# A two-layer hybrid attention network: squares and weight halves on VectorE, products of zeros ahead of the data, gates summed in four products

## The chip, the cores and the metric

The kernel runs on one core of a Trainium2 chip. TensorE (PE in the profile) multiplies matrices into PSUM, VectorE (DVE), ScalarE (ACT) and GpSimd (POOL) work on tiles, and SyncE (SP) and ACT issue the DMAs that bring data from HBM into SBUF. Each engine takes its own instructions in order and waits on semaphores of the others. The metric is the device time of one execution in microseconds (us); lower is better.

## The reference

A sequence of 512 tokens with 1024 features passes two layers, all in float32. Each layer is an attention with three groups of heads and then a convolutional feed-forward net:

```python
def rmsnorm(x, g):
    return x * rsqrt(mean(x * x, axis=-1) + EPS) * g

for i in range(2):
    h = rmsnorm(x, ln1_g[i]) @ w_in[i]            # 1024 -> 2724 columns
    fq, fk, fv, ff, dq, dk, dv, c_q, c_kv, k_r = split(h)
    # fox: 4 heads of 64, causal; bias cum[q] - cum[k],
    #      cum = cumsum over tokens of log_sigmoid(ff + f_bias): the forget gates
    # diff: 4 heads, softmax(q1 k1) v - lam * softmax(q2 k2) v, then a norm
    # mla: 4 heads, queries and keys from two low-rank latents, rotary part
    x = x + concat(o_fox, o_diff, o_mla) @ w_o[i]
    up = causal_dwconv(rmsnorm(x, ln2_g[i]) @ w_up[i])   # 1024 -> 2 x 2816, width 3
    x = x + (silu(up[:, :2816]) * up[:, 2816:]) @ w_down[i]
return rmsnorm(x, final_g)
```

## The kernel before

The activations lie transposed in eight tiles x0 to x7, 128 features by 512 tokens each. To keep float32 accuracy on fast products, every operand is split into a high half (`hi`, a copy on ACT in the reduced format) and a low half (`lo`, the rest, subtracted on DVE or POOL); `mm3` then makes three products: hi by hi, hi by lo, lo by hi. Weights come from HBM as float32 chunks (`raw`, three buffers) and are cut into pieces whose halves are called `whi` and `wlo`. `weights()` hands out the next piece and keeps the cutting two pieces ahead (`CUT_AHEAD`); four buffers each of `whi` and `wlo` turn. The second half of each `w_fm` chunk has its `wlo` made by POOL, every other `wlo` is DVE's (line 298).

A norm is not applied ahead of the product. `Norm.halves` splits x times its column factors; the factor of each token (one over the root of the mean square) is multiplied in afterwards. For it, ACT squares each x tile (`sq`), POOL adds the eight squares (`square`), TensorE sums over partitions with a column of ones (`inv_rms`, tile `at<-ones,r`), DVE and POOL take the root (`vn`, `rsn`), TensorE spreads the factors over partitions with transposes (`spread`) and ACT copies them (tile `r`, `rb`).

The program of a layer: `tm(w_fx)` computes the fox values, the gates and the rotary keys, token by token, 292 columns wide: eight slices k of x, each with four token tiles and three products, 96 in all. At the start of layer 0 each slice waits for its DMA, its halves and its weights. Then come two projections of 24 products 512 wide (`stacked_queries`, `stacked_keys`), `tm(w_dv)` with 96 such products, in which `cumulate` puts the gates' sums, and the remaining projections, woven between the steps of the heads. The weaving follows a planner (`Plan`) that holds a cost for each operation and takes up the step whose inputs it believes ready; its costs differ for DVE and POOL, so moving an operation also changes the order in which the heads' steps stand. After the heads, the last two products per output tile are added to x (`x<-mm,x`), each followed by `halves` and `square` for the next norm. The feed-forward part starts with two tiles (`raw`, each 24 products) before the norm's factors must be there.

PSUM has eight banks: three `mm`, two `sc`, two `at`, one `o`. In the profile nearly all instructions carry line L133, the planner's helper (L135 in the changed kernel); they are told apart by their tiles.

## Time and profile before

| | us |
|---|---|
| median of 3 runs (1241.84 to 1244.34) | 1241.91 |
| the profiled execution | 1244.5 |
| its span, first to last instruction | 1242.7 |
| PE busy | 1210.6 |
| DVE busy | 815.0 |
| ACT busy | 665.0 |
| POOL busy | 288.4 |

The rows below come from that one execution. The span is 1.8 us shorter than the execution's time. A row names the engine, the line, the operation and the tiles (written<-read); "x24" counts instructions. PEld is TensorE's loading of weights, which runs beside PE. A wait is put down to the engine that released it last.

### The profile page before, as it was taken

To read this page: it belongs to the slowest core of one execution; us is meant where nothing else is said; L and a number is where in the kernel's file an instruction comes from. 1 tells how busy PE (TensorE), PEld (TensorE's weight loads), DVE (VectorE), ACT (ScalarE), POOL (GpSimd) and SP (SyncE) were. 2 spreads that over 40 slices of the span, in tenths; PEclk is the share of its full clock that TensorE was granted. 3 is DMA by queue.
4 is the path that set the end of the run, shared out by engine and by line. 5 is a ranking of instruction groups with operands and counts; after the bars stand their busy time and mean duration, and the time that the engine had idled before them with its cause. 6 is when DMAs were issued, how large, how long until landed. Compare 5 with 4: busy or idle time off the path is not lost.

```text
span 1242.7 us, 16525 instructions
## 1 busy us (share of the span) xinstructions
PE 1210.6 (97%) x5792; PEld 1010.2 (81%) x5792; DVE 815.0 (66%) x1632; ACT 665.0 (54%) x1323; POOL 288.4 (23%) x378
## 2 busy tenths in 40 slices
PE   6999999999999999999999999999999999999997
PEld 6878877878888888888898788788788888888886
DVE  5578778687665357665554887887767643666743
ACT  5477777565543245444454776875545422454524
POOL 4165353141110001111123636322211100011102
PEclk8999999999999999999999999999999999999999
DMA  5211110222222332223232111113222233222231
GB/s 208 94 68 69 56 51 26 95 78 95 99 92 83 98 119 102 86 86 94 86 115 82 69 65 44 48 38 102 86 102 98 68 101 124 87 100 102 86 118 68
DMA packets 34356, 108.33 MB, mean 87 GB/s; under 512 B 3808, under 2 KB 3936, under 8 KB 34272
## 3 DMA queue, kind: packets, MB, share of 16 engines
q1 hardware_dynamic: 33984, 106.81, 25.8%
q8 instruction: 45, 0.74, 0.2%
q10 hardware_dynamic: 288, 0.47, 0.1%
q14 instruction: 39, 0.32, 0.1%
HBM read 105.16 MB, written 2.10 MB: 86 GB/s over the span
## 4 chain that ended last, share of the span: by engine, by line
PE 86%; DVE 6%; POOL 3%; ACT 2%; issue 2%; DMA 0%; POOLq 0%; DVEq 0%; ACTq 0%
PE mm L133 75%; PE sc L133 5%; PE at L133 4%; DVE a L133 2%; PE o L133 2%; POOL rq L133 1%; POOL wlo L133 1%; DVE row L133 1%; DVE wlo L133 1%; DVE w L133 1%; ACT a L133 1%; DVE x L133 1%; POOL row L133 1%; ACT row L133 0%; ACT u L133 0%
## 5 line engine op out<-in xcount | busy, mean ns | idle before, releaser
L133 PE MATMUL mm<-a,whi 128*128 128x512 f32 x2800 | 872.5, 392 | 4.4 <-DVE a L133 4.4
L133 PEld LDWEIGHTS mm<-a,whi 128*128 128x128 f32 x2800 | 520.7, 188 | 108.7 <-DVE a L133 5.8
L133 PE MATMUL mm<-a,wlo 128*128 128x512 f32 x1400 | 546.1, 390 | 0.0
L133 ACT ACTIVATE whi<-raw 128x512 fp32r<-128x512 f32 (+3 forms) x426 | 248.9, 585 | 373.2 <-PE mm L133 323.9
L133 DVE TENSOR_TENSOR wlo<-raw,whi 128x512 fp32r<-128x512 f32 (+3 forms) x396 | 260.6, 660 | 132.2 <-ACT whi L133 127.2
L133 PEld LDWEIGHTS mm<-a,wlo 128*128 128x128 f32 x1400 | 262.9, 188 | 54.4
L133 POOL TENSOR_TENSOR a<-w,a 128x512 fp32r<-128x512 f32 x44 | 57.2, 1300 | 540.6 <-ACT a L133 521.4
L133 DVE SCALAR_TENSOR_TENSOR w<-u,par_sb,w 128x511 f32<-128x511 f32 (+1 forms) x176 | 132.1, 750 | 32.0 <-ACT w L133 28.9
L133 DVE TENSOR_TENSOR u<-mm,r 128x512 f32<-128x512 f32 x88 | 60.9, 692 | 107.3 <-PE mm L133 107.3
L133 ACT ACTIVATE a<-w 64x512 fp32r<-64x512 f32 (+1 forms) x124 | 78.4, 632 | 43.4 <-DVE w L133 41.8
L133 ACT ACTIVATE w<-u,par_sb 128x512 f32<-128x512 f32 x88 | 71.9, 817 | 33.1 <-DVE u L133 33.1
L133 POOL TENSOR_SCALAR row<-row,rsum 128x512 f32<-128x512 f32 (+1 forms) x96 | 58.0, 607 | 134.1 <-DVE rsum L133 132.4
L133 ACT ACTIVATE row<-row,nm 128x512 f32<-128x512 f32 (+1 forms) x96 | 53.8, 561 | 24.7 <-DVE nm L133 24.6
L133 PE MATMUL sc<-a 128*128 128x512 f32 (+7 forms) x288 | 66.9, 337 | 0.0
L133 DVE TENSOR_TENSOR x<-mm,x 128x512 f32<-128x512 f32 x64 | 43.9, 688 | 32.8 <-PE mm L133 32.5
L133 PE MATMUL mm<-whi,a 128*128 128x512 f32 (+2 forms) x176 | 56.1, 367 | 8.8 <-ACT whi L133 6.5
L133 POOL TENSOR_TENSOR r<-r,w 128x512 f32<-128x512 f32 x28 | 41.7, 1489 | 93.0 <-ACT w L133 92.0
L133 POOL TENSOR_TENSOR wlo<-raw,whi 128x512 fp32r<-128x512 f32 x30 | 39.9, 1329 | 82.2 <-ACT whi L133 82.1
L133 DVE TENSOR_TENSOR pl<-at,ph 128x128 fp32r<-128x128 f32 (+1 forms) x96 | 45.7, 484 | 7.8 <-ACT ph L133 7.0
L133 PEld LDWEIGHTS sc<-a 128*128 128x128 f32 (+1 forms) x288 | 46.2, 191 | 5.5 <-DVE nm L133 0.8
L133 ACT ACTIVATE ph<-at 128x128 fp32r<-128x128 f32 (+1 forms) x96 | 40.6, 433 | 15.7 <-PE at L133 11.3
L133 PE MATMUL at<-c_sb,row 128*128 128x128 f32 x240 | 43.0, 278 | 4.5 <-POOL row L133 1.9
(139 smaller groups left out, 1075.5 us busy)
## 6 DMA issues: line engine op xcount, KB each, us to landing
raw<-in_w_up SPq DMA_DIRECT2D x88, 512.0 KB, 3.2
raw<-in_w_fm SPq DMA_DIRECT2D x30, 512.0 KB, 3.2
raw<-in_w_dn SPq DMA_DIRECT2D x24, 384.0 KB, 3.0
raw<-in_w_dn SPq DMA_DIRECT2D x24, 320.0 KB, 2.8
raw<-in_w_o SPq DMA_DIRECT2D x16, 384.0 KB, 2.9
raw<-in_w_dv SPq DMA_DIRECT2D x8, 512.0 KB, 3.2
raw<-in_w_dn SPq DMA_DIRECT2D x8, 512.0 KB, 3.5
raw<-in_w_fx SPq DMA_DIRECT2D x8, 292.0 KB, 3.7
```

The costliest lines, as they stand in the source:

```text
L133: return real(*args, **kw)
```

## The change

Seven edits:

- All `wlo` are made by DVE, and so are the sums of squares; POOL keeps neither.
- Ahead of any data DVE clears a tile `rest`, and TensorE makes eight products of zeros (512 wide) into the `o` bank.
- The first norm's column factors come by a DMA of their own (`g_sb`, 4 KB) at the place of the whole parameter block; that block (`par_sb`) and the constants (`c_sb`) are issued by SP after the `w_fx` products are recorded. x1 and the second weight chunk are issued by ACT, behind its table load and first copy.
- Squares are no longer tied to the halves. In `tm(w_fx)` they come from slice 4 on; the rest of them stand in the first projection, and the sums and the spreading come later in it than before.
- The accumulators of `tm(w_fx)` take banks sc, sc, o, mm.
- The feed-forward part makes three tiles first (two in sc, one in mm), with four squares after slice 3 of the first, four after its slice 7, the sums in slice 1 and the spreading in slice 6 of the third.
- The gates' running sums take four products per layer, 16, 12, 8 and 4 columns wide, in slice 5, at the place of ten products of 4 columns in slices 1 to 4.

```diff
--- before.py
+++ after.py
@@ -45,6 +45,8 @@
 FM_ORDER = [0, 2, 1, 3, 4, 8, 5, 9, 6, 10, 12, 13, 14, 7, 11]
 CUT_AHEAD, CUT_BUFS = 2, 4
 WIDTH, SLACK = 2, -1.5
+
+WARM = 8
 
 
 def lam_init_of(l):
@@ -229,13 +231,16 @@
 
         x = [cp.tile([P, S], F32, name=f"x{j}") for j in range(KD)]
         c_sb = cp.tile([P, NCST], F32, name="c_sb")
+        g_sb = cp.tile([P, KD], F32, name="g_sb")
         par_sb = cp.tile([P, NPAR], F32, name="par_sb")
         mhalf = cp.tile([P, NT], F32, name="mhalf")
         ones = cp.tile([P, 2], F32, name="ones")
 
+        nc.scalar.dma_start(g_sb, par[:, O_LN1:O_LN1 + KD])
+        rest = A()
+        nc.vector.memset(rest.bitcast(F32), 0.0)
         nc.gpsimd.memset(ones, 1.0)
         nc.gpsimd.memset(mhalf, -0.5)
-        nc.scalar.dma_start(par_sb, par)
         warm = small(2, "warm")
         nc.scalar.activation(warm, ones, AF.Copy)
 
@@ -269,19 +274,21 @@
         pieces = [(i, sum(ws[:b]), w) for i, (_, ws) in enumerate(chunks) for b, w in enumerate(ws)]
         state = {"load": 0, "cut": 0, "use": 0}
 
-        def load():
+        def load(queue=nc.sync):
             src, ws = chunks[state["load"]]
             raw = plan.tile("raw", 3, lp.tile([P, 1024], F32, name="raw", tag="raw"))[:, :sum(ws)]
             plan.written[raw.tensor.name] = plan.written[raw.tensor.name][0] + 3.6, "DVE"
-            nc.sync.dma_start(raw, src)
+            queue.dma_start(raw, src)
             raws[state["load"]] = raw
             state["load"] += 1
 
         for j in range(KD):
-            nc.sync.dma_start(x[j], xT[j * P:(j + 1) * P, :])
-            if j in (0, 2, 4):
-                load()
-        nc.sync.dma_start(c_sb, cst)
+            (nc.scalar if j == 1 else nc.sync).dma_start(x[j], xT[j * P:(j + 1) * P, :])
+            if j in (0, 1, 3):
+                load(nc.scalar if j == 1 else nc.sync)
+        idle = o_ps()
+        for _ in range(WARM):
+            nc.tensor.matmul(idle, lhsT=rest[:, :P], rhs=rest, start=True, stop=True)
 
         def ahead():
 
@@ -295,8 +302,7 @@
                 else:
                     hi, lo = (plan.tile(v, CUT_BUFS, lp.tile([P, S], F32R, name=v, tag=v, bufs=CUT_BUFS))[:, :w] for v in ("whi", "wlo"))
                 nc.scalar.activation(hi, src, AF.Copy)
-                eng = nc.gpsimd if off and chunks[i][0].tensor.name == w_fm.tensor.name else nc.vector
-                eng.tensor_tensor(out=lo, in0=src, in1=hi.bitcast(F32), op=ALU.subtract)
+                nc.vector.tensor_tensor(out=lo, in0=src, in1=hi.bitcast(F32), op=ALU.subtract)
                 ready.append((hi, lo))
                 state["cut"] += 1
 
@@ -360,7 +366,7 @@
             def halves(self, j):
                 self.xs.append(split(x[j], scale=self.g(j)))
 
-            def square(self, eng=None):
+            def square(self):
                 j = self.squares
                 self.squares += 1
                 sq = R() if j == 0 else W()
@@ -368,18 +374,19 @@
                 if j == 0:
                     self.acc = sq
                 else:
-                    (eng or nc.gpsimd).tensor_tensor(out=self.acc, in0=self.acc, in1=sq, op=ALU.add)
+                    nc.vector.tensor_tensor(out=self.acc, in0=self.acc, in1=sq, op=ALU.add)
 
             def ready(self, k):
 
                 while len(self.xs) <= min(k, KD - 1):
                     self.halves(len(self.xs))
-                    if len(self.xs) > 2:
-                        self.square()
+
+            def squares_to(self, n):
+                while self.squares < n:
+                    self.square()
 
             def sums(self):
-                while self.squares < KD:
-                    self.square()
+                self.squares_to(KD)
                 self.rs = inv_rms(self.acc, D, "n")
 
             def spread(self):
@@ -587,8 +594,8 @@
                     return ps
                 return f
 
-            def tm(w, width, between=lambda k: None):
-                acc = [mm_ps(), mm_ps(), sc_ps(), sc_ps()]
+            def tm(w, width, banks, between=lambda k: None):
+                acc = [bank() for bank in banks]
                 for k in range(KD):
                     norm.ready(k + 1)
                     hi, lo = weights(width, w)
@@ -607,11 +614,15 @@
 
 
             norm.ready(0)
-            acc = tm(w_fx, TMX)
+            acc = tm(w_fx, TMX, (sc_ps, sc_ps, o_ps, mm_ps), lambda k: norm.squares_to(max(0, k - 3)))
+            if l == 0:
+                nc.sync.dma_start(par_sb, par)
+                nc.sync.dma_start(c_sb, cst)
             first = stacked_queries(FM_ORDER[0])
+            next(first), norm.squares_to(KD)
+            next(first), next(first)
+            norm.sums()
             next(first)
-            norm.sums()
-            next(first), next(first)
             norm.spread()
             for _ in first:
                 pass
@@ -649,14 +660,12 @@
             cum_ps = at_ps()
 
             def cumulate(k):
-                qt = k - 1
-                if not 0 <= qt < NT:
+                if k != 5:
                     return
-                for t in range(qt + 1):
-                    c = C_TRI if t == qt else C_ONE
-                    nc.tensor.matmul(cum_ps[:, 4 * qt:4 * qt + 4], lhsT=c_sb[:, c:c + P], rhs=lf[:, 4 * t:4 * t + 4], start=t == 0, stop=t == qt)
-                if qt == NT - 1:
-                    nc.vector.tensor_copy(cum, cum_ps[:, 0:nz])
+                nc.tensor.matmul(cum_ps[:, 0:nz], lhsT=c_sb[:, C_TRI:C_TRI + P], rhs=lf, start=True, stop=False)
+                for t in range(1, NT):
+                    nc.tensor.matmul(cum_ps[:, 4 * t:nz], lhsT=c_sb[:, C_ONE:C_ONE + P], rhs=lf[:, 0:nz - 4 * t], start=False, stop=t == NT - 1)
+                nc.vector.tensor_copy(cum, cum_ps[:, 0:nz])
 
             def rotate(dst, src, cs, sn, shape, name):
 
@@ -680,7 +689,7 @@
             rotate(krr.rearrange("p (t o d) -> p t o d", t=NT, o=1), kr.rearrange("p (t o d) -> p t o d", t=NT, o=1), cs4, sn4, [P, NT, 1, hf], "ro")
 
 
-            acc = tm(w_dv, S, cumulate)
+            acc = tm(w_dv, S, (mm_ps, mm_ps, sc_ps, sc_ps), cumulate)
             dv = []
             for t in range(NT):
                 dv.append(split(acc[t], scale=rs1[:, t:t + 1]))
@@ -917,35 +926,36 @@
                     mm3(ps, (hi[:, c], lo[:, c]), oT[6 + k], k == 0, k == 1)
                 nc.vector.tensor_tensor(out=x[j], in0=ps, in1=x[j], op=ALU.add)
                 nxt.halves(j)
-                nxt.square()
             return nxt
 
         def ffn(l, norm):
             last = l == DEPTH - 1
             nxt = None if last else Norm(lambda j: col(l + 1, O_LN1, j))
+            made = {}
+
+            def raw(ft, gu, bank=mm_ps, between={}):
+
+                ps = made[ft, gu] = bank()
+                for k in range(KD):
+                    if k % 4 == 0:
+                        hi, lo = weights(S, w_up)
+                    c = slice(k % 4 * P, (k % 4 + 1) * P)
+                    mm3(ps, (hi[:, c], lo[:, c]), norm.xs[k], k == 0, k == KD - 1)
+                    if k in between:
+                        between[k]()
+
+
+            raw(0, 0, sc_ps, {3: lambda: norm.squares_to(4), 7: lambda: norm.squares_to(KD)})
+            raw(0, 1, sc_ps)
+            raw(1, 0, mm_ps, {1: norm.sums, 6: norm.spread})
             for half in range(2):
                 hT = []
                 for ft in range(half * HALF, (half + 1) * HALF):
-                    y2, tiles = [], []
-
-                    def raw(ps):
-                        for k in range(KD):
-                            if k % 4 == 0:
-                                hi, lo = weights(S, w_up)
-                            c = slice(k % 4 * P, (k % 4 + 1) * P)
-                            mm3(ps, (hi[:, c], lo[:, c]), norm.xs[k], k == 0, k == KD - 1)
-                            if ft == 0 and k == 3 and len(tiles) == 2:
-                                norm.spread()
-
+                    y2 = []
                     for gu in range(2):
-                        if len(tiles) == gu:
-                            tiles.append(mm_ps())
-                            raw(tiles[-1])
-                        if norm.rb is None:
-                            norm.sums()
-                            tiles.append(mm_ps())
-                            raw(tiles[-1])
-                        ps = tiles[gu]
+                        if (ft, gu) not in made:
+                            raw(ft, gu)
+                        ps = made[ft, gu]
                         a = U()
                         nc.vector.tensor_tensor(out=a, in0=ps, in1=norm.rb, op=ALU.mult)
                         y = W()
@@ -1009,7 +1019,7 @@
                 nc.vector.tensor_scalar(out=xt[t, 1], in0=xt[t, 1], scalar1=rs, scalar2=None, op0=ALU.mult)
                 nc.sync.dma_start(out[t * P:(t + 1) * P, S:D], xt[t, 1])
 
-        norm = Norm(lambda j: col(0, O_LN1, j))
+        norm = Norm(lambda j: g_sb[:, j:j + 1])
         for l in range(DEPTH):
             norm = attention(l, norm)
             norm = ffn(l, norm)
```

Where instructions stand before and after, by engine. First DVE in `tm(w_fx)` of layer 0, from the low half of slice 5 on (a: low halves of x; wlo: low halves of weights; vn: start of the root). Before:

```order
L133 SCALAR_TENSOR_TENSOR a_235<-x5_99,par_sb_103,a_234 128x512
L133 SCALAR_TENSOR_TENSOR a_260<-x6_100,par_sb_103,a_259 128x512
L133 SCALAR_TENSOR_TENSOR a_283<-x7_101,par_sb_103,a_282 128x512
L133 TENSOR_TENSOR wlo_244<-raw_146,whi_243 128x292
L133 TENSOR_TENSOR wlo_267<-raw_146,whi_266 128x292
L133 TENSOR_TENSOR wlo_292<-raw_193,whi_291 128x512
L133 TENSOR_TENSOR wlo_327<-raw_241,whi_326 128x512
L133 TENSOR_SCALAR vn_347<-at_342 128x4
```

and now, where r is the sum of squares and w a square:

```order
L135 SCALAR_TENSOR_TENSOR a_238<-x5_99,g_sb_103,a_237 128x512
L135 TENSOR_TENSOR r_247<-r_247,w_269 128x512
L135 TENSOR_TENSOR wlo_244<-raw_157,whi_243 128x292
L135 SCALAR_TENSOR_TENSOR a_262<-x6_100,g_sb_103,a_261 128x512
L135 TENSOR_TENSOR r_247<-r_247,w_294 128x512
L135 TENSOR_TENSOR wlo_266<-raw_157,whi_265 128x292
L135 SCALAR_TENSOR_TENSOR a_285<-x7_101,g_sb_103,a_284 128x512
L135 TENSOR_TENSOR r_247<-r_247,w_313 128x512
L135 TENSOR_TENSOR wlo_291<-raw_199,whi_290 128x512
L135 TENSOR_TENSOR r_247<-r_247,w_343 128x512
L135 TENSOR_TENSOR wlo_310<-raw_199,whi_309 128x512
```

Before, three slices' low halves stood ahead of the weights' of slices 6 and 7, and the sums were on POOL; now the weights' halves alternate with the slices, and the sums lie between them on the same engine.

Second DVE where layer 0's attention ends and its feed-forward part begins (a_3338 and a_3353, now a_3328 and a_3340, are the low halves of slices 6 and 7). Before:

```order
L133 SCALAR_TENSOR_TENSOR a_3319<-x5_99,par_sb_103,a_3318 128x512
L133 TENSOR_TENSOR x7_101<-mm_3344,x7_101 128x512
L133 SCALAR_TENSOR_TENSOR a_3338<-x6_100,par_sb_103,a_3337 128x512
L133 TENSOR_TENSOR wlo_3363<-raw_3221,whi_3362 128x512
L133 SCALAR_TENSOR_TENSOR a_3353<-x7_101,par_sb_103,a_3352 128x512
L133 TENSOR_TENSOR wlo_3379<-raw_3221,whi_3378 128x512
L133 TENSOR_TENSOR wlo_3407<-raw_3290,whi_3406 128x512
L133 TENSOR_SCALAR vn_3399<-at_3394 128x4
```

and now:

```order
L135 SCALAR_TENSOR_TENSOR a_3312<-x5_99,par_sb_104,a_3311 128x512
L135 TENSOR_TENSOR x7_101<-mm_3331,x7_101 128x512
L135 SCALAR_TENSOR_TENSOR a_3328<-x6_100,par_sb_104,a_3327 128x512
L135 TENSOR_TENSOR wlo_3347<-raw_3228,whi_3346 128x512
L135 SCALAR_TENSOR_TENSOR a_3340<-x7_101,par_sb_104,a_3339 128x512
L135 TENSOR_TENSOR r_3362<-r_3362,w_3364 128x512
L135 TENSOR_TENSOR wlo_3374<-raw_3228,whi_3373 128x512
L135 TENSOR_TENSOR r_3362<-r_3362,w_3367 128x512
L135 TENSOR_TENSOR wlo_3405<-raw_3286,whi_3404 128x512
L135 TENSOR_TENSOR r_3362<-r_3362,w_3370 128x512
L135 TENSOR_TENSOR wlo_3421<-raw_3286,whi_3420 128x512
```

The halves and x keep their order; the sums of squares (r_3362), which stood on POOL beside these, follow the last slice's half on DVE.

Third TensorE in `tm(w_dv)`, the last of the gates' sums (lf: logarithms of the gates; at: their sums). Before (groups of one, two and three stand in the three slices ahead of it):

```order
L133 MATMUL sc_489<-whi_509,a_187 128x512
L133 MATMUL sc_490<-whi_509,a_186 128x512
L133 MATMUL sc_490<-wlo_510,a_186 128x512
L133 MATMUL sc_490<-whi_509,a_187 128x512
L133 MATMUL at_475<-lf_472,c_sb_102 128x4 x4
L133 MATMUL mm_487<-whi_528,a_211 128x512
```

and now, the only group:

```order
L135 MATMUL sc_503<-whi_540,a_217 128x512
L135 MATMUL sc_503<-wlo_541,a_217 128x512
L135 MATMUL sc_503<-whi_540,a_218 128x512
L135 MATMUL at_488<-lf_485,c_sb_102 128x16
L135 MATMUL at_488<-lf_485,c_sb_102 128x12
L135 MATMUL at_488<-lf_485,c_sb_102 128x8
L135 MATMUL at_488<-lf_485,c_sb_102 128x4
L135 MATMUL mm_500<-whi_556,a_237 128x512
```

Ten products became four, one slice later. Beyond these places, the order of the heads' steps among the projections differs from the fox heads on, since the planner's view of DVE and POOL has changed.

## Rows read from the trace of the kernel before

**Rows 1.** The page, section 1: busy us (share of the span) xinstructions.

```profile
PE 1210.6 (97%) x5792; PEld 1010.2 (81%) x5792; DVE 815.0 (66%) x1632; ACT 665.0 (54%) x1323; POOL 288.4 (23%) x378
```

**Rows 2.** What TensorE waited for, whole span: us in total, times, longest us.

```profile
PE mm L133 <- DVE a L133: 4.8, 3, 2.2
PE mm L133 <- DVE wlo L133: 3.1, 1, 3.1
```

**Rows 3.** Stages of the start: us, busy (x) by engine, PEclk, DMA share, GB/s.

```profile
6.40:11.40 5.00, 4.95 (x20) 4.95 (x21) 4.47 (x7) 5.00 (x11) 2.28 (x2) 1.00 1.06 405
11.40:17.20 5.80, 5.80 (x44) 5.57 (x42) 5.80 (x5) 5.39 (x12) 5.00 (x5) 1.00 0.65 254
17.20:22.40 5.20, 1.74 (x12) 1.50 (x11) 5.20 (x5) 1.18 (x3) 4.75 (x3) 0.92 0.21 80
22.40:28.40 6.00, 5.99 (x24) 6.00 (x25) 1.62 (x3) 0.63 (x1) 0.00 (x0) 0.50 0.49 178
```

**Rows 4.** Timeline of the start: start us, us, instruction xcount [idle before <-releaser].

```profile
0.72 0.10 POOL L133 MEMSET ones<- 128x2 f32 x1 [0.29 <-POOLq L1068]
...
4.82 0.72 ACT L133 ACTIVATE a<-x,par_sb 128x512 fp32r<-128x512 f32 x1 [2.17 <-DMA par_sb<-in_par]
...
5.45 0.61 ACT L133 ACTIVATE r<-x 128x512 f32<-128x512 f32 x1
...
6.45 0.86 PE L133 MATMUL mm<-whi,a 128*128 128x292 f32 x2 [6.45 <-ACT whi L133]
...
7.38 0.75 DVE L133 SCALAR_TENSOR_TENSOR a<-x,par_sb,a 128x512 fp32r<-128x512 f32 x1
...
13.90 6.46 POOL L133 TENSOR_TENSOR r<-r,w 128x512 f32<-128x512 f32 x4 [0.47 <-ACT w L133]
...
15.76 5.15 DVE L133 SCALAR_TENSOR_TENSOR a<-x,par_sb,a 128x512 fp32r<-128x512 f32 x3
...
22.41 0.61 PE L133 MATMUL mm<-wlo,a 128*128 128x292 f32 x1 [3.07 <-DVE wlo L133]
```

**Rows 5.** The same timeline of TensorE, further on.

```profile
28.17 0.75 PE L133 MATMUL mm<-a,whi 128*128 128x512 f32 x2
```

**Rows 6.** DMA issues, first 22 us: xcount, KB each, median us to landing.

```profile
x<-in_xT SPq DMA_DIRECT2D x8, 256.0 KB, 5.3
...
c_sb<-in_cst SPq DMA_DIRECT2D x1, 832.0 KB, 7.1
par_sb<-in_par ACTq DMA_DIRECT2D x1, 200.0 KB, 4.1
```

**Rows 7.** Timeline, DVE, where layer 0's attention meets its feed-forward half.

```profile
264.32 1.78 DVE L133 TENSOR_TENSOR wlo<-raw,whi 128x512 fp32r<-128x512 f32 x1
266.02 1.74 DVE L133 SCALAR_TENSOR_TENSOR a<-x,par_sb,a 128x512 fp32r<-128x512 f32 x1
```

**Rows 8.** The same stretch, POOL.

```profile
257.14 10.08 POOL L133 TENSOR_TENSOR r<-r,w 128x512 f32<-128x512 f32 x6 [0.87 <-ACT w L133]
```

**Rows 9.** The same stretch, TensorE.

```profile
267.82 0.50 PE L133 MATMUL mm<-a,whi 128*128 128x512 f32 x1 [2.22 <-DVE a L133]
```

**Rows 10.** Chain that ended last, 40 to 60 us: shares by line.

```profile
by line: PE mm L133 51.1%; PE sc L133 41.0%; PE at L133 9.1%
```

**Rows 11.** Attention of layers 0 and 1; columns as in Rows 3.

```profile
66.00:256.00 190.00, 184.98 (x984) 154.16 (x983) 147.14 (x412) 133.94 (x341) 81.23 (x134) 1.00 0.18 60
674.00:864.00 190.00, 185.02 (x984) 154.16 (x983) 148.71 (x412) 135.28 (x341) 80.53 (x134) 1.00 0.18 60
```

**Rows 12.** POOL groups: xcount | busy us, mean ns | idle before.

```profile
L133 POOL TENSOR_SCALAR row<-row,rsum 128x512 f32<-128x512 f32 (+1 forms) x96 | 58.0, 607 | 134.1 <-DVE rsum L133 132.4 <-PE mm L133 1.3
...
L133 POOL TENSOR_TENSOR r<-r,w 128x512 f32<-128x512 f32 x28 | 41.7, 1489 | 93.0 <-ACT w L133 92.0
L133 POOL TENSOR_TENSOR wlo<-raw,whi 128x512 fp32r<-128x512 f32 x30 | 39.9, 1329 | 82.2 <-ACT whi L133 82.1
```

**Rows 13.** DVE groups by shape; columns as in Rows 12.

```profile
L133 DVE TENSOR_TENSOR wlo<-raw,whi 128x512 fp32r<-128x512 f32 x248 | 174.2, 703 | 54.0 <-ACT whi L133 49.7 <-PE mm L133 2.7
```

## The prediction

> **What bounds the kernel now.** I read the page's busy shares first, then what TensorE waited for, then the stages of the start, the timelines around the waits, and the chain that ended last. TensorE is busy 97% of the span and every other engine at most 81% [rows 1], so only two things can shorten the run: TensorE's own idle or slow time, and work taken from it. Its idle time lies in few places. It does nothing until 6.45 us [rows 4]. It then waits 3.1 us once for a low half of a weight, and 4.8 us in three waits for low halves of x [rows 2]; two of those three are the 2.22 us where each layer's attention meets the feed-forward part [rows 9]. In each layer's attention it is idle 190 minus about 185, or 5.0 us [rows 11], spread over many short waits.
>
> The start costs more than its waits. `tm(w_fx)` has 96 products 292 wide; it begins at 6.45 and the next projection at 28.17 [rows 4, 5], so it takes 21.7 us. In the stretch 22.4 to 28.4 the granted clock is 0.50, the lower of the two levels (1.2 GHz), and 24 products take 6.0 us, 0.25 each; in 11.4 to 17.2 it is 1.00 (2.4 GHz) and 44 take 5.8, 0.132 each [rows 3]. The first 20 also took 5.0 us [rows 3], the pace of the lower level, though the column says 1.00 there. All 96 at the fast pace would take 12.7 us. The other 9 are 44 products at the slow pace (44 x 0.118 = 5.2) and 3.5 of waits. The waits are DVE's: three low halves of x take 5.15 us while POOL adds squares without a break, where one alone takes 0.75 [rows 4].
>
> **The start, part by part.** ACT's first work waited for the parameter block (4.82), and a square stood between it and the first weights' half (5.45, 0.61 us) [rows 4]. The 4 KB of `g_sb` replace 200 KB [rows 6], which at the 405 GB/s of this stage [rows 3] are 0.5 us, and the square goes later: 6.45 - 0.5 - 0.55 (the square's pitch) makes the first product of data stand at 5.4. The zeros don't hold it up: engines begin at 0.72 [rows 4], clearing `rest` costs about what a 512-wide DVE operation does (0.70 [rows 13]), and eight products at 0.25 x 512/292 = 0.44 run from 1.5 to 5.0. If that is 0.4 too early, the first product moves by as much.
>
> Slice 0 has one chunk and one x tile ahead of it. Slice 1's x tile now comes by ACT's queue, issued behind ACT's table load and sharing the 405 GB/s with x2: 512 KB more after x0 and the first chunk (in by 4.9), so both are in at 6.2, and with a high half (0.72), a low half (0.75) and two weight halves of 0.4 (0.70 x 292/512) between, slice 1 can start at 8.2. From there a slice needs 256 + 146 KB, 1.0 us at 405 GB/s, against TensorE's 12 x 0.132 = 1.6; the constants' 832 KB [rows 6], 2.1 us, have left the queue ahead of the last chunk. DVE needs 8 x 0.75 + 8 x 0.4 + 3 sums x 0.7 = 11.3 us from 4.9 on, so it is done by 16 or 17, ahead of TensorE's last slice. So neither supply nor DVE bounds slices 1 to 7 any more; the 3.5 us of waits go, and the three sums are hidden by TensorE's products (if DVE were stretched as before, they cost the old 3.1 back).
>
> What decides is the clock. Before, the pace rose 4.9 us after products began (6.45 to 11.4) and again 6.0 us after 22.4 [rows 3, 4]. If the zeros count and the short gap behind them doesn't, it rises at 6.4 to 7.5; slice 1's start then binds, and the end is 8.2 + 84 x 0.132 = 19.3. If it counts from 5.4, it rises at 10.3 to 11.4: (11.4 - 5.4)/0.25 = 24 products are done, and the end is 11.4 + 72 x 0.132 = 20.9 (20.4 for 10.3). I take 20.1, between the two. So this term is 20.1 - 28.17 = -8.1, with -8.9 and -7.3 as ends, and -5 if ACT's queue brings x1 and its chunk 2.3 us late.
>
> The sums now follow 18 products of the next projection, 18 x 0.232 = 4.2 us after the end; DVE has four sums and four 512-wide weight halves left by then, 8 x 0.7 = 5.6 from about 17, so they are ready at 22.6 against 24.3. The spreading stands six products (1.4 us) behind them and may wait a few tenths; I put +0.2.
>
> **The seam of attention and feed-forward part.** The last slice's low half ran from 266.02 to 267.76 and the weights' half ahead of it took 1.78 [rows 7], all beside POOL's six sums, 10.08 us without a break [rows 8]; alone they take 0.75 and 0.70 [rows 4, 13]. These two alone give back 2.07 us, and the slices' halves ahead of them ran beside the same sums. With POOL silent I expect the wait of 2.22 to go whole, in both layers: -4.4 (at least -2 x 2.0; at most what is there). What is late next is nothing: the sums stand behind the last half on DVE, seven times 0.7 with weights' halves between, about 9 us, and TensorE needs them only after 54 products x 0.232 = 12.5 us. The three tiles wait for their factors in banks that nothing else wants by then.
>
> **The gates.** The chain gives the small products of ten 4-column sums 9.1% of 20 us, 1.82 [rows 10], with TensorE never waiting between; four of them cost 0.73 if a wider one costs the same. No row shows one of 16 columns; if all four blocks of 4 cost what they do now, nothing is saved. I take the first, the count of instructions being what goes: -1.1 per layer, -2.2 in all; ends 0 and -2.2. The sums come one slice later; their reader stands behind the last slice.
>
> **Weights' low halves on DVE.** 26 of the 30 belong to the woven part, 13 per layer: POOL needs 1.33 for one [rows 12], DVE 0.70 [rows 13], so 9.1 us per layer more on DVE, whose 147 of 190 us become 156, 82%. That is beside TensorE as long as a half is ready before its piece: it is cut two pieces ahead, 2 x 12 x 0.232 = 5.6 us. The heads' steps also stand in another order. I price both at 0, the nearest row being that layer 1 waits as long as layer 0; the ends are -10 (all 5.0 per layer gone) and +5 (half as much again).
>
> **The sum**: -8.1 + 0.2 - 4.4 - 2.2 = -14.5, and 1244.5 - 14.5 = 1230.0. The profiled execution is 2.6 above the median shown (1241.91), about what the slow stretch 22.4 to 28.4 cost (24 x 0.118 = 2.8). So against the median the gain is 11.9 us. The Trainium skill (TensorE: Matmul & The Clock Gate, Part 1: The HAM clock gate) says that one kernel shows different counts of slow products from run to run; the spread of the three runs agrees in size, and by it either end of the start may be met, 1229.2 or 1230.8.
>
> **Rivals.**
> 1. The new order makes the heads wait more: half as much again, +2.5 per layer, 1235. For it: DVE rises to 82%. Against: POOL, which ends some waits, becomes free, and a low half is there 0.6 sooner. 15%.
> 2. Slower than before: DVE falls behind in the woven part by more than the 5.6 us of lead, and from that point TensorE waits for each of the 26 halves, 26 x 0.70 = 18: 1248. For it: POOL's 96 `row` operations of 0.61 [rows 12] stay beside them. Against: DVE has 43 of 190 us free. 5%. The Trainium skill (SBUF — State Buffer, Who interferes with whom) speaks for it: a DVE instruction with two SBUF inputs and a GpSimd one that reads SBUF exclude each other, the later one standing still. The trace agrees in part: 1.74 for 0.75 beside sums of 1.7.
> 3. The start gains only -5, since x1 is late or the clock comes later than 11.4: 1233. 12%.
> 4. The seam's wait stays, since DVE's own order, not POOL, sets it: 1244.5 - 10.1 = 1234.4. Against: 2.07 of it stand in two rows. 5%.
> 5. The waits in attention halve, -5: 1225. For it: both engines that end them are relieved of each other. 8%.
>
> **How the numbers follow.** The forecast has 55% and reaches from 1227 to 1233. The range 1224 to 1237 adds rivals 1, 3, 4 and 5. About 0.2% is what a measurement of this kernel can tell from no change, so faster means under 1239.4: 0.92; within: 0.04, from the upper edge of rivals 1 and 4 together; slower: 0.04, from rival 2.
>
> **What would show it.** The first projection's first product at 19 to 21 (before 28.17), with one rise of the clock and no fall; DVE's low halves in slices 5 to 7 at 0.75; no wait where the seam was; one group of four small products per layer at about 0.7 us; TensorE's idle time in 66 to 256, shifted by some 9, at 5 or less. The forecast is wrong if the clock falls again behind the zeros, or if idle time in the heads goes beyond 8 us per layer.

## The result, and the profile after

The changed kernel takes 1220.16 us (median of four runs, 1220.01 to 1221.81) against 1241.88; the ratio is 0.9823, with a 95% interval of 0.9806 to 0.9840. The forecast was 1230.0 with a range of 1224 to 1237: the sign was right, and the gain is 21.7 us where 11.9 were expected. The kernel before varies from execution to execution together with its mean granted clock (in the runs further on, 1240.1 us at 0.999 to 1247.7 at 0.991); the traced one is 2.6 us above the median, so the spans of the two traces differ by 24.4.

Page of the changed kernel, section 1, and what TensorE waited for in the whole span (us in total, times, longest), to be held against [rows 1, 2]:

```profile
PE 1205.1 (99%) x5776; PEld 1005.2 (83%) x5776; DVE 822.1 (67%) x1691; ACT 661.9 (54%) x1323; POOL 208.1 (17%) x320
```

```profile
PE sc L135 <- DVE nm L135: 1.6, 2, 0.8
PE o L135 <- DVE a L135: 1.4, 1, 1.4
PE at L135 <- POOL row L135: 0.9, 2, 0.4
PE at L135 <- DVE pl L135: 0.8, 2, 0.4
PE at L135 <- POOL rsd L135: 0.2, 1, 0.2
```

The four waits of [rows 2] are gone, and what is left of waits for other engines is 4.9 us in all; the 1.4 for `DVE a` is the zeros' own wait for their cleared tile. TensorE's busy time fell by 5.5 us too, which a shorter idle time alone would not do.

Where the 24.4 us of span (1242.7 to 1218.3) lie is read from the starts of the same products in the two traces. Both programs issue 4656 products that read a half of a weight, in the same sequence but for 24 places (four in the first slice, ten in the heads of each layer), none of them at a row of the table. So the n-th of them is the same work before and after:

| n-th such product | before | after | ahead by | gained in between |
|---|---|---|---|---|
| 0, first projection | 6.45 | 5.36 | 1.09 | |
| 96, next projection | 28.17 | 18.94 | 9.23 | start: 9.23 |
| 144, `tm(w_dv)` | 40.58 | 31.41 | 9.17 | |
| 264, behind `w_dv` | 72.62 | 62.09 | 10.53 | gates, layer 0: 1.36 |
| 720, end of the woven part | 246.80 | 232.46 | 14.34 | heads, layer 0: 3.81 |
| 888, feed-forward part | 288.82 | 272.02 | 16.79 | seam: 2.45 |
| 2328, near its end | 615.22 | 598.42 | 16.79 | 0 |
| 2640, layer 1, behind `w_dv` | 684.02 | 665.92 | 18.10 | gates: 1.31 |
| 3100, end of the woven part | 858.39 | 836.44 | 21.95 | heads, layer 1: 3.85 |
| 3264, feed-forward part | 899.48 | 875.06 | 24.42 | seam: 2.47 |
| 4655, last | 1214.77 | 1190.35 | 24.42 | 0 |

So: start 9.2 (forecast 8.1), gates 2.7 (2.2), seam 4.9 (4.4), and 7.7 us in the woven parts of the heads, which the sum had priced at 0. The wait that the sum put behind the later norm sums (0.2) shows as 0.06.

TensorE at the start (start us, us, instruction, count), for [rows 4, 5]:

```profile
1.44 3.78 PE L135 MATMUL o<-a 128*128 128x512 f32 x8 [1.44 <-DVE a L135]
5.36 0.86 PE L135 MATMUL sc<-whi,a 128*128 128x292 f32 x2
...
6.94 0.29 PE L135 MATMUL sc<-wlo,a 128*128 128x292 f32 x1
...
7.74 0.29 PE L135 MATMUL sc<-whi,a 128*128 128x292 f32 x1
...
18.94 0.63 PE L135 MATMUL mm<-a,whi 128*128 128x512 f32 x2
```

and the same four stretches as in [rows 3]:

```profile
6.40:11.40 5.00, 5.00 (x38) 5.00 (x37) 4.50 (x10) 4.83 (x10) 0.00 (x0) 1.00 1.06 403
11.40:17.20 5.80, 5.80 (x45) 5.80 (x44) 5.80 (x11) 5.80 (x13) 0.00 (x0) 1.00 1.00 369
17.20:22.40 5.20, 5.20 (x31) 4.57 (x30) 3.66 (x9) 2.29 (x4) 0.00 (x0) 1.00 0.50 171
22.40:28.40 6.00, 6.00 (x33) 4.91 (x32) 3.12 (x9) 2.58 (x6) 1.54 (x2) 1.00 0.15 60
```

The zeros run from 1.44; five products of data go at the slow pace (the first 0.41 us to the next, the others 0.24 to 0.25, the pace of the lower level of 1.2 GHz), and from 6.9 they follow each other at 0.13. Nothing falls back: the clock column stays at 1.00 (2.4 GHz), where it was 0.50 at the end of the start before. POOL is silent and DVE's busy share in the third stretch is down from 5.20 to 3.66 of 5.2.

DVE at the seam of layer 0, for [rows 7]:

```profile
248.42 0.69 DVE L135 TENSOR_TENSOR wlo<-raw,whi 128x512 fp32r<-128x512 f32 x1
249.02 0.75 DVE L135 SCALAR_TENSOR_TENSOR a<-x,par_sb,a 128x512 fp32r<-128x512 f32 x1
249.68 0.68 DVE L135 TENSOR_TENSOR r<-r,w 128x512 f32<-128x512 f32 x1
```

The low half that took 1.74 takes 0.75, and the weight's half 0.69 in place of 1.78, with the sums of squares (`r<-r,w`) now on the same engine behind them; no row answers [rows 8], since POOL has nothing in that stretch, nor [rows 9], since TensorE doesn't wait there. The heads, in the stretches that hold the same 984 products as those of [rows 11] (columns as above), take 186.2 us in place of 190, with TensorE busy 184.25, so idle 1.95 where it was 5.0:

```profile
55.50:241.70 186.20, 184.25 (x984) 153.88 (x983) 151.53 (x424) 134.03 (x341) 65.31 (x121) 1.00 0.19 61
655.90:842.10 186.20, 184.25 (x984) 153.89 (x983) 151.06 (x424) 135.27 (x341) 65.34 (x121) 1.00 0.19 61
```

POOL's busy time fell by 15.9 and 15.2, and DVE's rose by 4.4 and 2.4 only, where 9.1 were expected. The stretches hold 11 of POOL's low halves each, not 13, and DVE's other operations got shorter: its 24 `a<-w,a` took 0.79 and 0.84 each before and take 0.70 now.

### The profile page after: what moved, and what is told of

Same layout as the page of the kernel before. It is cut to its first block, busy times and chain, and to the rows that moved or that the text cites. A ratio compares the mean times of both kernels' runs of the same rounds, so it can differ in the third digit from the quotient of the medians.

```text
span 1218.3 us, 16462 instructions
## 1 busy us (share of the span) xinstructions
PE 1205.1 (99%) x5776; PEld 1005.2 (83%) x5776; DVE 822.1 (67%) x1691; ACT 661.9 (54%) x1323; POOL 208.1 (17%) x320
## 4 chain that ended last, share of the span: by engine, by line
PE 93%; POOL 2%; DVE 2%; ACT 2%; issue 1%; DMA 0%; POOLq 0%; SPq 0%; ACTq 0%; DVEq 0%
PE mm L135 78%; PE sc L135 8%; PE at L135 4%; PE o L135 3%; POOL b L135 1%; DVE w L135 1%; ACT u L135 1%; ACT row L135 0%; POOL row L135 0%; DVE a L135 0%; DVE row L135 0%; DMA raw<-in_w_fx 0%; ACT a L135 0%; POOL rsd L135 0%; ACT w L135 0%
## 5 line engine op out<-in xcount | busy, mean ns | idle before, releaser
L135 PE MATMUL mm<-a,whi 128*128 128x512 f32 x2736 | 850.9, 392 | 0.0
L135 PEld LDWEIGHTS mm<-a,whi 128*128 128x128 f32 x2736 | 508.4, 188 | 101.8 <-DVE a L135 0.4
L135 PE MATMUL mm<-a,wlo 128*128 128x512 f32 x1368 | 533.2, 390 | 0.0
L135 DVE TENSOR_TENSOR wlo<-raw,whi 128x512 fp32r<-128x512 f32 (+3 forms) x426 | 272.8, 641 | 126.8 <-ACT whi L135 122.0
L135 PEld LDWEIGHTS mm<-a,wlo 128*128 128x128 f32 x1368 | 256.8, 188 | 53.5
L135 DVE SCALAR_TENSOR_TENSOR w<-u,par_sb,w 128x510 f32<-128x510 f32 (+1 forms) x176 | 133.0, 761 | 28.0 <-ACT w L135 25.3
L135 DVE TENSOR_TENSOR u<-mm,r 128x512 f32<-128x512 f32 x84 | 58.0, 691 | 98.9 <-PE mm L135 98.9
L135 PE MATMUL mm<-whi,a 128*128 128x512 f32 (+2 forms) x144 | 46.7, 363 | 0.0
L135 POOL TENSOR_SCALAR b<-r,cum 128x128 f32<-128x128 f32 (+2 forms) x56 | 28.8, 527 | 63.4 <-ACT r L135 42.9
L135 ACT ACTIVATE w<-w 128x512 f32<-128x512 f32 x50 | 31.7, 634 | 14.4 <-DVE w L135 11.5
```

The lines of the kernel that those rows point to most:

```text
L135: return real(*args, **kw)
```

## The experiments

All times are medians of four runs (ten for the run of constant subtractions); the kernel before ran beside them at 1244.2 to 1244.9, wider spread than at first (1240.0 to 1247.7). They are compared with the changed kernel, which ran once more beside (4), (6) and (7). Where an edit leaves a part alone, the starts of its products agree with the changed kernel's to about 0.1 us in the heads; the end of the first projection lies between 18.4 and 19.3 in the traces of runs that do not aim at it, so differences at the start are known to about 0.5. Diffs leave lines out where they show "...".

> The changed kernel once more, unchanged, as the base of the three runs beside it: 1220.2 us by every theory.

It took 1220.04.

### Order or engine, in the woven part

Moving a low half does two things: another engine makes it, and the planner, which sets the order of the heads' steps from where it believes each piece is made, writes another order. Three kernels complete the square with the changed one; in the woven parts TensorE's sequence in (1) and (2) is that of the kernel before, and in (3) that of the changed kernel, instruction for instruction:

(1) POOL makes the second halves of `w_fm`, and is planned so:

```diff
-                nc.vector.tensor_tensor(out=lo, in0=src, in1=hi.bitcast(F32), op=ALU.subtract)
+                eng = nc.gpsimd if off and chunks[i][0].tensor.name == w_fm.tensor.name else nc.vector
+                eng.tensor_tensor(out=lo, in0=src, in1=hi.bitcast(F32), op=ALU.subtract)
```

> The changed kernel, but POOL makes the low halves of w_fm's second half again, in the order of instructions that the kernel before had in the woven part; start, gates and seam stay changed. The changed kernel takes 1220.2 us; 7.65 us of its gain lie in the two woven parts (3.8 per layer). Theory E (the engine: a half is ready sooner on VectorE, or POOL is freed): the 7.65 come back, 1227.8. Theory O (the order of the heads' steps, which the planner sets from where it believes the halves are made): they come back too, 1227.8. Rival N (they come from another edit, such as a shift of the stages against the DMAs): 1220.2.

(2) planned for POOL, made by DVE:

```diff
-                nc.vector.tensor_tensor(out=lo, in0=src, in1=hi.bitcast(F32), op=ALU.subtract)
+                eng = Engine(plan, "POOL", tc.nc.vector) if off and chunks[i][0].tensor.name == w_fm.tensor.name else nc.vector
+                eng.tensor_tensor(out=lo, in0=src, in1=hi.bitcast(F32), op=ALU.subtract)
```

> The changed kernel, but the planner is told that POOL makes the 30 low halves, so that the heads' steps stand in the order of the kernel before, while VectorE makes them. Theory E (the engine): 1220.2 us, as the changed kernel. Theory O (the order): the 7.65 us of the woven parts come back, 1227.8. With both at work the time lies between, and this run and its counterpart with the two roles exchanged share the 7.65 between them.

(3) planned for DVE, made by POOL:

```diff
-                nc.vector.tensor_tensor(out=lo, in0=src, in1=hi.bitcast(F32), op=ALU.subtract)
+                eng = Engine(plan, "DVE", tc.nc.gpsimd) if off and chunks[i][0].tensor.name == w_fm.tensor.name else nc.vector
+                eng.tensor_tensor(out=lo, in0=src, in1=hi.bitcast(F32), op=ALU.subtract)
```

> The changed kernel with every engine's order of the heads' steps kept, but the 30 low halves are made by POOL, which the planner does not know. Theory E (the engine): the 7.65 us of the woven parts come back, 1227.8. Theory O (the order): 1220.2, as the changed kernel. A mismatch of both (an order planned for one engine, work done by the other) may cost more than either: above 1227.8.

They took 1227.22, 1222.06 and 1224.10. The starts of the same products give what the two woven parts alone cost above the changed kernel's:

| | DVE makes them | POOL makes them |
|---|---|---|
| order of the changed kernel | 0 (1220.0) | 4.2 (1224.1) |
| order of the kernel before | 1.8 (1222.1) | 7.2 (1227.2) |

Neither theory stands alone. The engine is worth 4.2 to 5.4, the order 1.8 to 3.0, and together they are 7.2 of the 7.7 us that the forecast missed; the other 0.4 is not accounted for. What TensorE waited for in (1) and in (2) shows the two parts:

```profile
PE at L135 <- DVE pl L135: 2.5, 4, 0.8
PE at L135 <- POOL row L135: 1.9, 5, 0.6
PE mm L135 <- DVE v L135: 1.9, 2, 0.9
PE at L135 <- ACT u L135: 1.5, 2, 0.7
```

```profile
PE mm L135 <- DVE v L135: 1.9, 2, 1.0
PE at L135 <- POOL row L135: 1.3, 4, 0.4
PE at L135 <- ACT u L135: 1.1, 2, 0.5
```

With DVE making the halves the wait of 2.5 for `DVE pl` goes and those for POOL's `row` shrink; the waits for `DVE v` (0.9 per layer) and `ACT u` belong to the old order, and in the changed order, (3) included, they do not occur at all. None of the four lists a wait in the heads for a low half.

### What POOL's halves cost: its time or its reads

POOL is given work beside the halves that DVE makes, outside the plan, so that the orders of the woven parts stay but for one place per layer in (4) and two in (5), where a clearing of a tile `a` and a `row`, both POOL's, change places. (4) makes each half a second time:

```diff
...
+                if off and chunks[i][0].tensor.name == w_fm.tensor.name:
+                    tc.nc.gpsimd.tensor_tensor(out=spare[:, :w], in0=src, in1=hi.bitcast(F32), op=ALU.subtract)
```

> The changed kernel, and in the two woven parts POOL makes each of the low halves of w_fm's second half a second time, into a spare tile that nothing reads (30 subtractions of 1.3 us that wait for the same high half); every engine's order is kept. With POOL making the halves instead of VectorE in this order the two woven parts took 4.2 us longer (the gap between that run and the changed kernel, from the starts of the same products). Theory H (a half was there later, or VectorE's 0.70 in place of 1.33 is the gain): 1220.2. Theories W, Q and C (POOL stands waiting for ScalarE's high half, its other work queues behind the 1.3 us, or its reads slow VectorE): 1224.4.

(5) clears, held to its place by one column of the high half:

```diff
...
+                if off and chunks[i][0].tensor.name == w_fm.tensor.name:
+                    tc.nc.gpsimd.tensor_copy(spare[:, :1], hi[:, :1].bitcast(F32))
+                    for part in (spare, spare, spare[:, :256]):
+                        tc.nc.gpsimd.memset(part, 0.0)
```

> The changed kernel, and in the woven parts, at the places of the 30 low halves, POOL copies one column of the high half (which holds it to its place) and then clears spare tiles for 1.3 us; it reads nothing else. The run with a second subtraction by POOL at these places took 1230.0 against 1220.0. Theory Q (time on POOL: its own later work comes later): 1230. Theory C (a subtraction that reads two tiles in SBUF slows VectorE, and that is the cost): 1220.2. Both at work: between, and the distance to 1220 is the queue's part.

(4) took 1229.99, 9.7 us of it in the woven parts, twice what was expected; (5) took 1228.07, 7.6 of it there. Theory H falls: in both DVE makes the halves when it did, and the time goes all the same. Time on POOL almost without the reads costs four fifths of what it costs with them. Clearing and its copy hold POOL 1.7 us a place in the woven parts, the subtraction 1.4; scaled to the same time on POOL (an estimate) the share is two thirds. So POOL's time carries most of it. In (5):

```profile
PE at L135 <- POOL row L135: 3.2, 4, 1.3
PE at L135 <- DVE pl L135: 2.8, 4, 1.0
```

Both (4) and (5) also hold POOL until ScalarE's high half is there, so their times do not separate theory Q from theory W. The trace of (5) does. Half of layer 0's delay arises between 64 and 73 us, POOL and TensorE there:

```profile
63.22 1.25 POOL L135 TENSOR_SCALAR row<-row,rsum 128x512 f32<-128x512 f32 x2
64.43 0.63 POOL L308 COPY spare<-whi 128x1 f32<-128x1 f32 x1
65.12 1.11 POOL L310 MEMSET spare<- 128x512 f32 x2
...
72.23 0.66 PE L135 MATMUL at<-c_sb,row 128*128 128x128 f32 x4 [1.25 <-POOL row L135]
```

POOL goes from its own work into the copy without a pause and stays busy until it releases TensorE, so nothing was lost there by waiting for the high half: it is the queue. Most of the layer's other half arises behind 158 us, and there too the copy follows POOL's own work without a pause. The reads add the rest: in (4) DVE's low halves of weights in the woven parts take 0.762 each on average, in (5) 0.674, in the changed kernel 0.665.

That also says why moving 1.3 us of POOL costs only 4.2 in (3) and 9.7 in (4): there DVE has the halves as well. Beside a DVE that makes the halves, sparing POOL is worth 9.7; beside a POOL that makes them, loading DVE costs 5.5. The prediction had only DVE's side in view, and half of a sentence on POOL.

(6) is (5) without the copied column:

```diff
...
+                if off and chunks[i][0].tensor.name == w_fm.tensor.name:
+                    for part in (spare, spare, spare[:, :256]):
+                        tc.nc.gpsimd.memset(part, 0.0)
```

> The changed kernel, and at the same 30 places POOL clears spare tiles for about 1.3 us, which waits for nothing and reads nothing. Theory Q (POOL's other work, the row operations above all, queues behind 1.3 us): 1224.4 us. Theory W (POOL stands waiting for ScalarE's high half) and theory C (POOL's reads of SBUF slow VectorE): 1220.2. Theory H (the halves were late): 1220.2.

(7) subtracts a constant tile:

```diff
...
+                if off and chunks[i][0].tensor.name == w_fm.tensor.name:
+                    tc.nc.gpsimd.tensor_tensor(out=spare, in0=still, in1=still, op=ALU.subtract)
```

> The changed kernel, and at the same 30 places POOL subtracts a constant tile from itself into a spare one, 128x512, about 1.3 us, which waits for nothing but reads two operands in SBUF as the low half does. Theory Q (the queue on POOL): 1224.4 us. Theory C (its reads slow VectorE's operations that read two tiles): 1224.4, with VectorE's a<-w,a back at 0.84 us from 0.70. Theory W (POOL's waiting for ScalarE) and theory H: 1220.2.

These two took 1224.07 and 1239.39, but not where they were meant to act: held by nothing, the 30 operations ran one after the other from the span's beginning to about 53 and 43 us, and the woven parts were as in the changed kernel (to 0.1 us). For the question asked they show nothing, and that (6) meets the 1224.4 of theory Q is chance: its 3.9 us arise between 18.9 and 62, where its instructions stand in another order too, in a wait of 2.2 for DVE's `w` and a stretch at the lower clock behind it (0.57 for 3 us). For the start they are the sharpest test there is, since POOL is busy through the whole first projection in both, once writing alone, once reading. DVE in (6), then in (7):

```profile
10.73 0.75 DVE L135 SCALAR_TENSOR_TENSOR a<-x,g_sb,a 128x512 fp32r<-128x512 f32 x1
11.39 0.45 DVE L135 TENSOR_TENSOR wlo<-raw,whi 128x292 fp32r<-128x292 f32 x1
12.02 0.75 DVE L135 SCALAR_TENSOR_TENSOR a<-x,g_sb,a 128x512 fp32r<-128x512 f32 x1 [0.18 <-ACT a L135]
```

```profile
11.69 1.30 DVE L135 TENSOR_TENSOR wlo<-raw,whi 128x292 fp32r<-128x292 f32 x1
12.91 1.52 DVE L135 SCALAR_TENSOR_TENSOR a<-x,g_sb,a 128x512 fp32r<-128x512 f32 x1
```

Beside clearing DVE keeps its 0.75 and 0.45; beside POOL's subtractions (1.14 to 1.37 each) the same operations take 1.52 and 1.30, and the first projection's end moves from 18.9 to 29.7. TensorE's waits for DVE's `a` and `wlo` are 8.6 us of that; between them its products follow each other at 0.13. The Trainium skill (SBUF — State Buffer, Who interferes with whom) says that a VectorE instruction with two inputs in SBUF contends with a GpSimd one that reads SBUF, and not with one that only writes it. Both halves of that rule agree with these rows. The prediction had named that rule only as a rival, against the change.

### The sums of squares

```diff
-                    nc.vector.tensor_tensor(out=self.acc, in0=self.acc, in1=sq, op=ALU.add)
+                    nc.gpsimd.tensor_tensor(out=self.acc, in0=self.acc, in1=sq, op=ALU.add)
```

> The changed kernel with the sums of squares on POOL again, at the places where the changed kernel has them. Theory C (beside POOL's sums VectorE's low halves of x take 1.7 in place of 0.75): the wait at the seam of attention and feed-forward part returns, 2 x 2.2 to 2.5, and the first projection takes 1 to 3 us more: 1225.5 to 1228, with the low halves of x beside the sums at 1.5 to 1.8 us. Rival (the seam was set by VectorE's own order, not by POOL): 1220.2.

It took 1228.44. The start is 2.0 us longer, the seam 2.5 in layer 0 and 4.0 in layer 1. DVE and TensorE at the seam of layer 0:

```profile
251.88 1.78 DVE L135 TENSOR_TENSOR wlo<-raw,whi 128x512 fp32r<-128x512 f32 x1
253.58 1.74 DVE L135 SCALAR_TENSOR_TENSOR a<-x,par_sb,a 128x512 fp32r<-128x512 f32 x1
```

```profile
255.38 0.50 PE L135 MATMUL sc<-a,whi 128*128 128x512 f32 x1 [2.23 <-DVE a L135]
```

These are [rows 7, 9] again, to 0.01 us, in the changed kernel's order: the seam was POOL's sums, and the rival that DVE's own order set it falls. In layer 1 the same wait of 2.23 is followed by a stretch at the lower clock, which the other layer's was not (stretches behind the two waits):

```profile
255.40:258.00 2.60, 2.60 (x11) 2.15 (x12) 1.83 (x3) 0.63 (x1) 0.00 (x0) 1.00 0.33 109
...
858.20:861.00 2.80, 2.77 (x7) 2.19 (x8) 1.87 (x3) 0.63 (x1) 0.00 (x0) 0.50 0.40 120
```

### The zeros

```diff
-WARM = 8
+WARM = 0
...
-        rest = A()
-        nc.vector.memset(rest.bitcast(F32), 0.0)
...
-        idle = o_ps()
```

> The changed kernel without the eight products of zeros and the tile that they read; all else stays. Theory of the clock (the zeros bring its rise forward): the rise comes 4.9 to 6.0 us after the first product of data at 5.36, at 10.3 to 11.4 us in place of 6.86, as it did before after 6.45 and after 22.4; slices 1 to 3 of the first projection then run at 0.25 us a product, and the run takes 1.5 to 2.0 us more, about 1221.9. Rival (the start is bound by the loads and by VectorE, and the zeros do nothing): 1220.2.

It took 1221.67, 1.6 more. The pace rises after 16 slow products in place of 5 (stretch from the first product to the rise, and from there to the next projection):

```profile
5.60:9.50 3.90, 3.90 (x16) 3.90 (x17) 3.59 (x7) 3.63 (x8) 0.00 (x0) 1.00 1.04 400
9.50:20.30 10.80, 10.80 (x82) 10.80 (x81) 10.53 (x21) 9.02 (x18) 0.00 (x0) 1.00 0.76 289
```

11 more products at 0.11 more each are 1.2, and the first one came 0.2 later; the next projection starts at 20.3, 1.1 us behind the latest of the runs that do not aim at the start. The rise came 3.9 us after the first product, sooner than the 4.9 to 6.0 that two stretches of the kernel before had shown. The column reads 1.00 over the slow stretch too, as it did in the first of [rows 3]. With the same eight zeros the rise itself is not fixed: in the eleven traces that have them the fast pace is there from the second or third product of data (5.5 to 5.8, five traces) or comes by 7.7 at the latest.

### The gates

```diff
             def cumulate(k):
-                if k != 5:
+                qt = k - 1
+                if not 0 <= qt < NT:
                     return
...
+                for t in range(qt + 1):
+                    c = C_TRI if t == qt else C_ONE
+                    nc.tensor.matmul(cum_ps[:, 4 * qt:4 * qt + 4], lhsT=c_sb[:, c:c + P], rhs=lf[:, 4 * t:4 * t + 4], start=t == 0, stop=t == qt)
...
```

> The changed kernel with the gates' sums in ten products of four columns again, group by group between the slices. By the starts of the same products before and after the change: 1.39 and 1.31 us per layer come back, 1222.7. By the prediction's price (1.1 a layer): 1222.2. If four wider products cost what ten narrow ones do: 1220.0.

It took 1228.90 (1227.66 to 1230.74), three times what any expectation said; the trace is of a run of 1229.92. What TensorE waited for, and the stretches around it in layer 0:

```profile
PE at L135 <- DVE lf L135: 4.6, 2, 2.3
```

```profile
36.00:38.30 2.30, 0.02 (x1) 0.05 (x1) 1.04 (x10) 2.25 (x5) 0.00 (x0) 1.00 0.41 162
38.30:41.50 3.20, 3.20 (x10) 2.62 (x10) 1.33 (x9) 1.63 (x3) 0.00 (x0) 0.51 0.00 0
41.50:45.00 3.50, 3.50 (x20) 2.98 (x19) 0.69 (x1) 0.63 (x1) 0.00 (x0) 0.96 0.23 84
```

With the norm's sums behind the first projection, `lf` is written at about 38, and ten products that begin behind slice 1 of `w_dv` stand there from 36.0. TensorE is still for 2.3 us, and the next 3.2 us run at a granted clock of 0.51 (1.2 GHz), ten products where the 3.5 us behind them hold twenty. Layer 0 loses 5.6 us by it and layer 1, whose wait of 2.3 no slow stretch follows, 4.0. So the move to slice 5 is more than four products for ten; it is what lets the sums of the norm come as late as the change puts them.

### A try at a better version

```diff
-WARM = 8
+WARM = 34
...
-            return max(0.108, n * 0.000418)
+            return max(0.108, n * 0.000443)
...
-        rest = A()
+        rest = A()[:, :P]
...
-            nc.tensor.matmul(idle, lhsT=rest[:, :P], rhs=rest, start=True, stop=True)
+            nc.tensor.matmul(idle[:, :P], lhsT=rest, rhs=rest, start=True, stop=True)
```

In the planner ScalarE's cost per column also became 0.001 and VectorE's 0.00122.

> A try at a better version: the changed kernel with the zeros begun earlier (34 products of 128 columns from a tile that is cleared in a quarter of the time) and the planner's costs set to what the profile shows (0.227 us for a 512-wide product, 0.59 for a high half, 0.69 for VectorE's 512-wide operations). The zeros: up to five slow products of the first slice become fast, 5 x 0.11 = 0.55 us less. The order: of 1.9 us idle per layer in the heads up to a half may go (-2 in all), or a worse order costs as much as the old one did (+3). 1217.6 to 1222.7; most likely 1219.5.

It took 1228.89 (1226.45 to 1231.03), worse by both edits (the trace is of a run of 1226.83; the 4 us more of two other runs are in no trace). The zeros begin at 1.03, but a product of 128 columns takes 0.22 at that pace, not a quarter of 0.47, and they keep TensorE from the data until 8.35:

```profile
1.03 7.51 PE L135 MATMUL o<-a 128*128 128x128 f32 x34 [1.03 <-DVE a L135]
8.35 0.55 PE L135 MATMUL sc<-whi,a 128*128 128x292 f32 x1
```

Nor did they bring the rise forward: twelve products of data still go at the slow pace, and the fast one begins at 11.35, 10.3 us after the first of the narrow zeros, where eight wide ones had it by 7.7 at the latest (stretches of the zeros, of the slow products of data and behind the rise):

```profile
1.03:8.35 7.32, 7.32 (x35) 7.32 (x35) 2.34 (x4) 4.02 (x8) 0.00 (x0) 1.00 0.92 318
8.35:11.35 3.00, 3.00 (x13) 3.00 (x14) 2.50 (x5) 3.00 (x7) 0.00 (x0) 1.00 0.95 337
11.35:22.55 11.20, 11.20 (x85) 11.20 (x85) 10.38 (x20) 8.46 (x17) 0.00 (x0) 1.00 0.66 238
```

The first projection ends 3.6 us later by it. Why the narrow products did not count is not shown.

By the starts of the same products the new order costs another 2.9 us, nearly all of it between the gates and the seam. Closer costs did not make a better plan. What is left in the changed kernel (under 2 us idle per layer in the heads) pointed to no other version.

## Why the prediction was wrong

1. **The step that failed** is "I price both at 0, the nearest row being that layer 1 waits as long as layer 0", on the woven part. Its two ends, -10 and +5, held the measured -7.7, but the value taken was read from a row that says nothing on it: two layers with the same order and the same engines wait alike whatever causes the waits. The rows that bore on it were the waits by cause. In the kernel before (not shown ahead of the prediction) they read

```profile
PE at L133 <- DVE pl L133: 2.9, 4, 0.9
PE mm L133 <- DVE v L133: 1.9, 2, 1.0
PE at L133 <- POOL row L133: 1.9, 4, 0.7
PE at L133 <- ACT u L133: 1.4, 2, 0.7
PE at L133 <- DVE row L133: 0.8, 2, 0.4
```

   These are 8.9 us in waits for the heads' own steps, none of them for a weight's half. The prediction asked whether a half would be ready in time, 0.70 against 1.33 with 5.6 us of lead, and that was never what TensorE waited for. It waited for steps that stood late because of POOL's queue behind the 30 halves of 1.33 [rows 12], and for steps that the order had put late (`DVE v`, `ACT u`). The experiments give the sizes: engine 4.2 to 5.4, of which POOL's time is the larger part, and order 1.8 to 3.0. Idle time fell by 3.1 and 3.0 in the two layers; the other 0.7 of each is counted as a shorter busy time of the same 984 products, and why it fell is not shown.

2. **Rival 5** (the waits halve, -5, 1225) came nearest to the mechanism, "both engines that end them are relieved of each other", and was given 8%. The engine that was loaded was weighed at length (82% busy foreseen, 81% measured), the one that became free in a word.

3. **Start**: right in kind, 9.2 for 8.1 and a little beyond the better end, 8.9. Two guesses had been averaged, and the first of them held: the zeros count, the pace rises at 6.9, slice 1 starts at 7.74 (8.2 forecast), and 7.74 + 84 x 0.132 = 18.83 against 18.94 measured. ACT's queue did not hold x1 behind the table load: it was issued at 1.23, while the load ran from 1.17 to 2.45, and landed at 5.06, ahead of x2 at 6.17. Of the 9.2, the zeros are worth 1.4 and POOL's silence 2.0 by one run each; the remaining 5.8 (loads, the first product 1.1 earlier, the fall of the clock that no longer comes) were not taken apart.

4. **Seam**: right; 2.45 and 2.47 for 2.22 each. The wait itself went whole; the 0.2 beside it were not taken apart.

5. **Gates**: 1.36 and 1.31 for 1.1. The small products went from 1.89 to 0.81 us, as counted. The other 0.3 lies in the wide products: the first one behind each group of small ones takes 0.32 to the next in place of 0.23, and there is one such group per layer where there were four. That the move of the sums was needed by the later norm went unseen.

6. **Range**: with the rest of the sum as measured (-16.8) the woven part's own ends would have reached down to 1217.7. The range stopped at 1224 because the ends of the unknown were entered as rivals, one at a time, while three other terms came out a little beyond their better ends together (9.2 for 8.9, 2.7 for 2.2, 4.9 for 4.4).

## What to carry to other kernels

When work moves from one engine to another, price both ends of the move: what stands behind it in the queue of the engine that is freed, beside what it costs the engine that takes it; the list of waits by cause, followed back along the chain, says which of the two TensorE has been waiting for. Where a planner orders the code, a change of engine is also a change of order, and one run with the planner told the old engine separates the two. Two edits that look independent may lean on each other, as the late sums of the norm and the late gates do here.

## What the runs showed of the hardware

- POOL's subtractions of two tiles in SBUF and DVE's two-input operations take turns one by one over a whole stretch of (7): DVE's start at 10.24, 11.69 and 12.91, POOL's at 10.08, 11.30 and 12.75. DVE's 0.75 became 1.52 and its 0.45 became 1.30, while POOL's own went from 1.04 (its shortest) to 1.14 beside the narrower and 1.37 beside the wider ones. Clearing by POOL left DVE's at 0.75.
- Of seven waits of TensorE of 2.2 to 2.3 us, three were followed by about 3 us at the lower clock: gates run, layer 0 (0.51), run with the sums on POOL, layer 1's seam (0.50), and (6) behind 33.6 us (0.57). Four were not (1.00): gates run, layer 1, sums run, layer 0's seam, and both seams of the kernel before.
- Ahead of the first rise of the clock a product of 128 columns took 0.22 us (34 in 7.51) and one of 512 columns 0.47 (8 in 3.78). The eight wide ones, 3.8 us long, brought the rise forward in all eleven traces; the 34 narrow ones, 7.5 us long, did not in the one trace that there is.
